# Six seven-product pairs in every block, and one PSUM bank used for two sums in turn

## The chip, the core and the metric

The kernel runs on one core of a Trainium2 chip. The metric is the device time of one execution in microseconds. The engines are called TensorE (PE), VectorE (DVE), ScalarE (ACT), GpSimd (POOL) and SyncE (SP); POOL and SP also issue transfers, each from a queue in order.

## The reference

Two layers of a bidirectional encoder on 256 tokens of width 4096, all in float32:

```python
for l in range(DEPTH):                       # DEPTH = 2
    h = rmsnorm(x, norm_w[l])
    proj = h @ w_in[l]                       # 4096 x 11264
    aq, ak, av, ag, rq, rk, rv, rg = jnp.split(proj, SPLIT_POINTS, axis=-1)
    a_out = silu(ag) * gqa_attention(rope(norm(aq)), rope(norm(ak)), av)       # 16 heads
    r_out = silu(rg) * rmsnorm(bidirectional_retention(rope(rq), rope(rk), rv)) # 8 heads
    x = x + jnp.concatenate([a_out, r_out], axis=-1) @ w_out[l]                # 4096 x 4096
return rmsnorm(x, final_norm)
```

Nearly all of the arithmetic is in the products with `w_in` and `w_out`.

## The kernel before, in words

**Blocks.** The columns of `w_in` are taken in 11 blocks of 1024 per layer and those of `w_out` in 4, so there are 30 blocks. The 4096 rows of a weight matrix are 16 *pairs* of 128-row slices (p = 0 to 15). In a block each pair contributes a 2 x 2 product of matrices: two halves of the tokens, two slices of the rows, two halves of the columns. It is done in eight products, or in Winograd's way in seven.

**A product** is brought close to float32 by three matmuls of 512 columns: the high parts of weights (`whi`) and operand (`x8h`, `x7h`), high by low, low by high. L1472 issues the two with the weights' high part, L1482 the one with the low part. A product is added into one of the sums M1 to M8, each in a PSUM bank; the eighth bank is called `ps` and belongs to attention and retention. M1 to M7 have a bank each.

**Seven or eight.** `SEVEN` lists the pairs done in seven products in the w_in blocks, `MORE` those added in the w_out blocks. The eight-product pairs use the sums of the others: `EIGHT_PRODUCTS` spreads them over M2 to M5, which needs the operand's difference (the *third* operand, `x3`, high and low). `PLAIN_PRODUCTS` needs no difference but a sum M8 of its own; with `plain` blocks M8 lies in `ps`. `NATIVE` pairs (1 and 0) are taken in the very first block as plain float32 matmuls (L1466), straight from the operand as it comes.

**Pages.** The weights of a pair are used as pages. An eight-product pair has pages A and B, of four products each. A seven-product pair has A, T, B and U, of 2, 2, 1 and 2 products; T and U are sums that DVE makes from the raw weights (`wsum`). For a page ACT makes `whi` and DVE makes `wlo`. `RING` = 5 pages are in work: when PE has used a page up, the fifth after it is begun. The raw weights come by SP's queue into `RAWS` buffers (L458). Pages of `FAR_PAIRS` (their B page) are *far*: ACT makes the high part and its negative, and POOL adds the raw weights to it by an accumulating transfer from DRAM (`flo`, L516); `FAR` buffers hold them. `pages_of` gives the order within a group, which is one seven-product pair and the eight-product pairs up to the next.

**Operands.** `split_pair` makes a pair's operand for a *stage* (in, out, in, out): high and low parts, for a seven-product pair also four sums and a negative (`xf`), for the others the third operand. The stage's inputs are the results of the stage before: chunks of two pairs, the last two of which (pairs 12 to 15) stay on the chip and come last. In stage 0 the thirds are made later (`DEFER`), after the `plain` blocks.

**The order of work** is written out by a planner inside the kernel while it is built. It keeps an estimate of PE's, DVE's and ACT's time and gives tasks (gates, rotary embedding, attention, retention, residual and norm) a place between the weights' work where `room` says that there is slack. `STEP_S`, `MARGIN`, `RUSH`, `EARLY`, `ADD_AHEAD`, `NEED`, `PE_REST`, `TIGHT_A`, `TIGHT_B`, `BANK_REST` and `SPLITS` are its constants. `PAGES` buffers of 4 KB per partition serve the tasks. At a block's end `combine` adds the banks into `ca` and `cb`; the sums of pair 15 are sorted to the end in `LAST_ORDER`. `TOGETHER` is how many products of a page have their high matmuls issued before their low ones.

**The start.** 20 warm-up matmuls run first (L1705). `first_rows(0)` loads the rows of x, transposed, for pair 1, then the first weights, then those for pair 0; ACT scales them (`full`, by `nw`) in the order of `NATIVE`, pair 1 before pair 0. In the order before, `pages_of` puts pair 1's pages ahead of pair 0's.

Of the kernel before, what the change touches and what calls it, by code (L numbers as in the profile page):

```python
# [17 lines left out]
P = 128  # L18
# [9 lines left out]
NB = 512  # L28
# [6 lines left out]
ALL = slice(None)  # L35
PAGES = 9
RAWS = 5

RING = 5
FAR = 1  # L40

STEP_V = 1.6
STEP_S = 1.3

# [9 lines left out]
FAR_LANDING = 11.0  # L54
MARGIN = 0.2

RUSH = 1.5

EARLY = 0.7

ADD_AHEAD = 2.5

NEED = {"ak": 4, "ag": 3, "rk": 4, "rg": 4}

PE_REST = 1.5

TIGHT_A = 4
TIGHT_B = 7

# [3 lines left out]

SPLITS = 3

START = 1

SEVEN = (0, 3, 6, 9, 12)

MORE = (1,)  # L80

# [5 lines left out]

PLAIN = 2

DEFER = (0,)  # L90

FAR_PAIRS = (2, 5, 8, 11, 14)

# [79 lines left out]
EIGHTS = [_p for _p in range(NP) if _p not in SEVENS[1]]  # L173

GROUPS = [[tuple(range(_a, _b)) for _a, _b in zip(_s, _s[1:] + (NP,))] for _s in SEVENS]


def pages_of(group, first=False):

    order, one = [], group[:1]  # L180
    rest = group[1:]
    if first:
        order += [(_p, _k) for _p in NATIVE if _p in group for _k in (PAGE_A, PAGE_B)]
        one = [_p for _p in one if _p not in NATIVE]
        rest = [_p for _p in rest if _p not in NATIVE]
    one = [(_p, _k) for _p in one for _k in (PAGE_A, PAGE_T, PAGE_B, PAGE_U)]
    rest = [(_p, _k) for _p in rest for _k in (PAGE_A, PAGE_B)]
    turns = TURNS if group[-1] == NP - 1 else "0123"
    for _i, _v in enumerate(one):
        order += [_v] + [rest.pop(0) for _j in turns if _j == str(_i) and rest]  # L190
    return order + rest
# [21 lines left out]

EASY = ("M7",)


BANK_REST = 0.8
APART = 0.0

TOGETHER = 4  # L220

OTHER = True

TURNS = "0123"

# [47 lines left out]
def hybrid_encoder(  # L273
# [318 lines left out]
    def dead_room():  # L592

        if not rooms:
            e, o = len(EIGHTS), len(SEVENS[1])
            kinds = {
                "x3": ("x3", e, [P, 2, 2, P], "p k s t -> p (k s t)"),
                "x8h": ("x8h", e, [P, 2, SEQ], "p k s -> p (k s)"),
                "x8l": ("x8l", e, [P, 2, SEQ], "p k s -> p (k s)"),
                "x7h": ("x7h", o, [P, 7, P], "p k t -> p (k t)"),  # L600
                "x7l": ("x7l", o, [P, 7, P], "p k t -> p (k t)"),
            }
            for p in range(NP):
                if p not in EIGHTS:
                    rooms.extend(kinds[v] for v in ("x7h", "x7l"))
                else:
                    rooms.extend(kinds[v] for v in ("x3", "x8h", "x8l")[: 3 if p in EIGHTS[2:] and p not in DELAYED else 1])
        tag, bufs, shape, flat = rooms.pop(0)
        return t(ap, shape, tag, bufs, F32R).rearrange(flat)[:, :NB]
# [18 lines left out]
    def split_pair(p, v, whole, stage):  # L628
# [39 lines left out]
        else:  # L668
            if p in EIGHTS:
                hi = t(ap, [P, 2, SEQ], "x8h", len(EIGHTS), F32R)  # L670
                lo = t(ap, [P, 2, SEQ], "x8l", len(EIGHTS), F32R)
                g = t(ap, [P, 2, 2, P], "x3", len(EIGHTS), F32R)
                g = [g[:, k] for k in range(2)]
            else:
                both = [t(ap, [P, 7, P], v, len(SEVENS[1]), F32R) for v in ("x7h", "x7l")]
                hi, lo = (v[:, 0:4, :].rearrange("p (i m) t -> p i (m t)", m=MT) for v in both)
                g = [v[:, 4:6, :] for v in both]
            g4 = [tokens(v) for v in g]
# [8 lines left out]
            for h, w, src in pieces:  # L687
                ve.tensor_sub(w, src, f32(h))
            if stage in DEFER:
# [671 lines left out]
    def block(after_pair, phase, then, first_order=False, order=LAST_ORDER, last=None, plain=False, hurried=False):  # L1361
# [12 lines left out]
        if plain:  # L1374
            order = PLAIN_ORDER
            bank[0] = True
# [11 lines left out]
        flat = [v for v in flat if not at_end(v)] + end  # L1388
        banks = BANKS if plain else BANKS[:-1]
        first = {b: next(i for i, v in enumerate(flat) if v[0] == b) for b in banks}  # L1390
# [5 lines left out]
        acc, pages, c = {}, {}, []  # L1396
        done = []
        def begin_product(n, name, p, index, k, h):
# [90 lines left out]
    def combine(bank, acc, c):  # L1489
# [109 lines left out]
    def last_combine(res):  # L1599
# [10 lines left out]
        def last(bank, acc, c):  # L1610
# [4 lines left out]
            if bank == "M6":  # L1615
                combine(bank, acc, c)
                ve.tensor_add(cb[:, 1, :], ca[:, 1, :], res[1, 1])
                ve.tensor_add(ca[:, 1, :], ca[:, 1, :], res[0, 1])
                ve.tensor_add(cb[:, 0, :], cb[:, 0, :], res[1, 0])
                ve.tensor_add(ca[:, 0, :], ca[:, 0, :], res[0, 0])  # L1620
            elif bank == "M2":
                combine(bank, acc, c)
                square(0, c, 0)
            elif bank == "M5":
                ve.tensor_add(cb[:, 0, :], cb[:, 0, :], acc["M5"])
                ve.tensor_add(cb[:, 1, :], cb[:, 1, :], acc["M5"])
                square(1, c, 1)
# [213 lines left out]
```

## Time and profile before

| | |
|---|---|
| time, median of 3 runs | 2622.15 us (2621.75 to 2622.28) |
| span of the profiled execution, first to last instruction | 2619.4 us, 2.75 us below the median of the runs; the page gives no other time for it |
| PE busy | 2599.9 us (99%), 11725 matmuls |
| DVE, ACT, POOL busy | 2168.9 (83%), 1805.0 (69%), 373.9 us (14%) |
| moved by DMA | 683.95 MB, mean 261 GB/s |
| granted clock of PE | 0.998 |

Matmuls are pipelined: the profile shows one of 512 columns as 0.39 us, but they start closer together than that, so a pace is read from start to start. `M` stands for all of M1 to M7. L258 is the helper through which all DVE and ACT work is issued, so its rows are told apart by their tiles.

### The profile page before, as it was taken

Reading aid. Unit: us, or ns where it says so; the run is one execution under the profiler, and the core shown is the slowest. Engines: PE = TensorE matmul, PEld = TensorE weight load, DVE = VectorE, ACT = ScalarE, POOL = GpSimd, SP = SyncE. Lnnn points to the kernel's source line nnn. Section 1 sums busy time; section 2 is a strip of 40 time slices with the busy share of each in tenths; the row PEclk is TensorE's granted clock in tenths of the full one; section 3 lists DMA queues with packets and bytes.
Section 4 is the critical chain, followed back from the end, with each engine's and each line's share of the span. In section 5 each row is a group of like instructions: output and inputs, shape, how many; then the busy total and the mean of one; then the engine's idle time right before and its main releaser. Section 6 shows DMA issues by size and latency. Waiting matters only on the chain.

```text
span 2619.4 us, 34550 instructions
## 1 busy us (share of the span) xinstructions
PE 2599.9 (99%) x11725; PEld 2153.7 (82%) x11725; DVE 2168.9 (83%) x2684; ACT 1805.0 (69%) x2576; POOL 373.9 (14%) x510
## 2 busy tenths in 40 slices
PE   9999999999999999999999999999999999999998
PEld 7888888888888888888878888888888888888886
DVE  8898887888778898877888878987887688987876
ACT  8766776666666788656886666776676567876555
POOL 0012221220111101111111111221110111010000
PEclk9999999999999999999999999999999999999999
DMA  8979989887878787988888888988877887788886
GB/s 306 292 257 297 284 257 287 274 270 240 247 229 258 225 252 237 283 269 269 301 251 262 271 286 268 278 270 282 280 228 218 249 259 237 224 255 270 242 261 221
DMA packets 201122, 683.95 MB, mean 261 GB/s; under 512 B 24176, under 2 KB 30832, under 8 KB 200944
## 3 DMA queue, kind: packets, MB, share of 16 engines
q1 hardware_dynamic: 147760, 521.27, 57.2%
q0 software_dynamic: 53184, 160.46, 26.3%
q8 instruction: 92, 1.51, 0.2%
q14 instruction: 86, 0.70, 0.1%
HBM read 637.60 MB, written 44.04 MB: 260 GB/s over the span
## 4 chain that ended last, share of the span: by engine, by line
PE 90%; DMA 1%; DVE 1%; issue 0%; ACT 0%; POOL 0%; POOLq 0%; DVEq 0%; ACTq 0%
PE M L1472 58%; PE M L1482 29%; PE ps L988 1%; PE ps L989 1%; PE ps L987 1%; DMA flo<-in_w_in 1%; DMA x7h<-in_w_out 0%; DVE wlo L258 0%; DVE ca L258 0%; DVE cb L258 0%; ACT flo L258 0%; ACT fhi L258 0%; ACT whi L258 0%; ACT x L258 0%; DVE xf L258 0%
## 5 line engine op out<-in xcount | busy, mean ns | idle before, releaser
L258 ACT CAST whi<-wraw 128x1024 fp32r<-128x1024 f32 (+1 forms) x808 | 768.0, 961 | 468.0 <-PE M L1472 318.7
L258 DVE TENSOR_TENSOR wlo<-wraw,whi 128x1024 fp32r<-128x1024 f32 (+1 forms) x808 | 887.6, 1110 | 234.0 <-ACT whi L258 226.2
L1472 PE MATMUL M<-whi,x8h 128*128 128x512 f32 x1340 | 521.8, 389 | 0.0
L1472 PE MATMUL M<-whi,x8l 128*128 128x512 f32 x1340 | 521.4, 389 | 0.0
L1472 PE MATMUL M<-whi,x7h 128*128 128x512 f32 x1265 | 493.2, 390 | 2.8 <-DVE ca L258 2.6
L1472 PE MATMUL M<-whi,x7l 128*128 128x512 f32 x1265 | 492.4, 389 | 0.0
L258 ACT CAST whi<-wsum 128x1024 fp32r<-128x1024 f32 x314 | 329.8, 1050 | 142.3 <-PE M L1472 109.2
L1482 PE MATMUL M<-wlo,x8h 128*128 128x512 f32 x1340 | 420.8, 389 | 0.0
L258 DVE TENSOR_TENSOR wlo<-wsum,whi 128x1024 fp32r<-128x1024 f32 x314 | 382.6, 1219 | 36.7 <-ACT whi L258 33.6
L1482 PE MATMUL M<-wlo,x7h 128*128 128x512 f32 x1265 | 408.5, 389 | 2.0 <-DVE wlo L258 2.0
L1472 PEld LDWEIGHTS M<-whi,x8l 128*128 128x128 f32 x1340 | 251.6, 188 | 52.3 <-issue 0.2
L1472 PEld LDWEIGHTS M<-whi,x8h 128*128 128x128 f32 x1340 | 251.5, 188 | 52.0 <-ACT full L258 0.2
L1482 PEld LDWEIGHTS M<-wlo,x8h 128*128 128x128 f32 x1340 | 250.5, 188 | 50.7
L1472 PEld LDWEIGHTS M<-whi,x7h 128*128 128x128 f32 x1265 | 237.5, 188 | 55.1 <-DVE ca L258 3.8
L1482 PEld LDWEIGHTS M<-wlo,x7h 128*128 128x128 f32 x1265 | 237.2, 188 | 51.6 <-DVE wlo L258 2.9
L1472 PEld LDWEIGHTS M<-whi,x7l 128*128 128x128 f32 x1265 | 237.5, 188 | 48.8
L1472 PE MATMUL M<-whi,x 128*128 128x512 f32 x840 | 258.8, 389 | 0.0
L516 POOL DMA_DIRECT2D flo<-in_w_in x108 | 96.7, 896 | 1045.3 <-ACT flo L258 965.6
L258 ACT CAST fhi<-wraw 128x1024 fp32r<-128x1024 f32 (+1 forms) x148 | 154.7, 1045 | 103.0 <-PE M L1472 97.7
L258 DVE TENSOR_TENSOR wsum<-wraw 128x1024 f32<-128x1024 f32 x157 | 191.2, 1218 | 24.2 <-DMA wraw<-in_w_out 15.6
L1472 PEld LDWEIGHTS M<-whi,x 128*128 128x128 f32 x840 | 156.9, 188 | 32.2 <-ACT whi L258 0.2
L1472 PE MATMUL M<-fhi,x8h 128*128 128x512 f32 x440 | 171.3, 389 | 0.0
(307 smaller groups left out, 3280.5 us busy)
## 6 DMA issues: line engine op xcount, KB each, us to landing
wraw<-in_w_in SPq DMA_DIRECT2D x700, 512.0 KB, 5.1
wraw<-in_w_out SPq DMA_DIRECT2D x256, 512.0 KB, 5.3
flo<-in_w_in POOLq DMA_DIRECT2D x108, 512.0 KB, 8.2
flo<-in_w_out POOLq DMA_DIRECT2D x38, 512.0 KB, 8.7
full<-next_dram POOLq DMA_DIRECT2D x18, 512.0 KB, 7.6
p_dram<-room POOLq DMA_DIRECT2D x64, 128.0 KB, 4.7
pT<-p_dram POOLq DMA_DIRECT2D x16, 512.0 KB, 5.9
next_dram<-room POOLq DMA_DIRECT2D x40, 128.0 KB, 6.8
```

What stands on the lines that cost most here:

```text
L258: return call(out, *args, **kwargs)
L516: nc.gpsimd.dma_start(g.lo[h], g.src[0][:, h, :], accum_op=ALU.add)
L987: nc.tensor.matmul(out, a[0], b[0], start=start, stop=False)
L988: nc.tensor.matmul(out, a[0], b[1], start=False, stop=False)
L989: nc.tensor.matmul(out, a[1], b[0], start=False, stop=stop)
L1472: nc.tensor.matmul(acc[name], a[i], g.hi[h], start=m == first[name] and not i, stop=False)
L1482: nc.tensor.matmul(acc[name], a, g.lo[h], start=False, stop=m == final[name])
```

## The change

Pairs 0, 1, 4, 5, 9 and 10 become the seven-product pairs in all blocks (before: 0, 3, 6, 9, 12 in w_in, and 1 as well in w_out). Eight-product pairs below `CUT` = 10 (2, 3, 6, 7, 8) keep `EIGHT_PRODUCTS` and a third operand. Those from 11 on use `PLAIN_PRODUCTS`. Their sum M8 takes M5's bank: when M5 is complete (pair 10), ACT copies it to a tile `m5`, and the bank is begun anew. Only the first block is wholly plain, with M8 in `ps` (before: two). The sums that are complete early are combined in the last 20 products. Far pages are those of seven pairs instead of five, in two places instead of one; raw buffers go from five to four and task buffers from nine to ten. In the last group the pages of pairs 11 to 15 come after all pages of pair 10.

```diff
-PAGES = 9
-RAWS = 5
+PAGES = 10
+RAWS = 4
-FAR = 1
+FAR = 2
-STEP_S = 1.3
+STEP_S = 1.5
-MARGIN = 0.2
-RUSH = 1.5
-EARLY = 0.7
-ADD_AHEAD = 2.5
-NEED = {"ak": 4, "ag": 3, "rk": 4, "rg": 4}
-PE_REST = 1.5
-TIGHT_A = 4
-TIGHT_B = 7
+MARGIN = 0.0
+RUSH = 2.0
+EARLY = 1.3
+ADD_AHEAD = 2.0
+NEED = {"ak": 5, "ag": 3, "rk": 4, "rg": 5}
+PE_REST = 1.2
+TIGHT_A = 0
+TIGHT_B = 3
-SPLITS = 3
-START = 1
-SEVEN = (0, 3, 6, 9, 12)
-MORE = (1,)
+SPLITS = 2
+START = 2
+SEVEN = (0, 1, 4, 5, 9, 10)
+MORE = ()
+CUT = 10
-PLAIN = 2
+PLAIN = 1
-FAR_PAIRS = (2, 5, 8, 11, 14)
+FAR_PAIRS = (2, 3, 7, 8, 11, 13, 15)
...
+CROSSED = [_p for _p in EIGHTS if _p < CUT]
...
-    turns = TURNS if group[-1] == NP - 1 else "0123"
     for _i, _v in enumerate(one):
-        order += [_v] + [rest.pop(0) for _j in turns if _j == str(_i) and rest]
+        order.append(_v)
+        if rest and _i >= (0 if rest[0][0] < CUT else TURN):
+            order.append(rest.pop(0))
...
-            eight = PLAIN_PRODUCTS if plain else EIGHT_PRODUCTS
+            eight = EIGHT_PRODUCTS if _p in CROSSED and not plain else PLAIN_PRODUCTS
...
-LAST_ORDER = ("M3", "M5", "M4", "M2")
-FINAL_ORDER = ("M5", "M2", "M3", "M4")
-PLAIN_ORDER = ("M3", "M8", "M4", "M2")
+LAST_ORDER = ("M3", "M8", "M4", "M2")
+FINAL_ORDER = ("M8", "M2", "M3", "M4")
+ENDING = 20
-BANK_REST = 0.8
+BANK_REST = 1.0
-TOGETHER = 4
+TOGETHER = 2
-TURNS = "0123"
+TURN = 3
...
             if n == first[name]:
-                acc[name] = t(pm, [P, NB], "ps" if name == "M8" else name)
+                if name == "M8" and not plain:
+                    now.wait(acc["m5_at"])
+                acc[name] = t(pm, [P, NB], name if name != "M8" else "ps" if plain else "M5")
...
-            if n == final[name]:
-                finished.append((name, partial(last or combine, name, acc, c)))
+            if n == final[name] and name == "M5" and not plain:
+                acc["m5"] = t(sp, [P, NB], "m5")
+                ac.copy(acc["m5"], acc["M5"])
+                acc["m5_at"] = ac.until + PASS
+            elif n == final[name]:
+                (finished if n >= len(flat) - ENDING else early).append((name, partial(last or combine, name, acc, c)))
+            if early and n >= len(flat) - ENDING:
+                finished.extend(early)
+                early.clear()
...
         if bank == "M6":
             ve.tensor_add(cb[:, 0, :], ca[:, 0, :], acc["M6"])
             ve.tensor_add(ca[:, 1, :], cb[:, 0, :], acc["M7"])
-            if "M8" in acc:
-                combine("M5 and M6", acc, c)
+            m5 = acc.get("m5", acc["M5"])
+            ve.tensor_add(cb[:, 1, :], ca[:, 1, :], m5)
+            ve.tensor_add(cb[:, 0, :], cb[:, 0, :], m5)
         elif bank == "M8":
             ve.tensor_add(cb[:, 1, :], cb[:, 1, :], acc["M8"])
-            free_bank()
-        elif bank == "M5 and M6" or bank == "M5" and "M8" not in acc:
-            ve.tensor_add(cb[:, 1, :], ca[:, 1, :], acc["M5"])
-            ve.tensor_add(cb[:, 0, :], cb[:, 0, :], acc["M5"])
+            if "m5" not in acc:
+                free_bank()
```

More of the change, by code (lines that the diff above doesn't have):

```diff
@@ L596, in dead_room @@
             kinds = {
-                "x3": ("x3", e, [P, 2, 2, P], "p k s t -> p (k s t)"),
+                "x3": ("x3", len(CROSSED), [P, 2, 2, P], "p k s t -> p (k s t)"),
                 "x8h": ("x8h", e, [P, 2, SEQ], "p k s -> p (k s)"),
@@ L605, in dead_room @@
                     rooms.extend(kinds[v] for v in ("x7h", "x7l"))
-                else:
-                    rooms.extend(kinds[v] for v in ("x3", "x8h", "x8l")[: 3 if p in EIGHTS[2:] and p not in DELAYED else 1])
+                elif p in EIGHTS[2:] and p not in DELAYED:
+                    rooms.extend(kinds[v] for v in ("x8h", "x8l"))
+                if p in CROSSED:
+                    rooms.append(kinds["x3"])
         tag, bufs, shape, flat = rooms.pop(0)
@@ L671, in split_pair @@
                 lo = t(ap, [P, 2, SEQ], "x8l", len(EIGHTS), F32R)
-                g = t(ap, [P, 2, 2, P], "x3", len(EIGHTS), F32R)
-                g = [g[:, k] for k in range(2)]
             else:
@@ L676, in split_pair @@
                 hi, lo = (v[:, 0:4, :].rearrange("p (i m) t -> p i (m t)", m=MT) for v in both)
-                g = [v[:, 4:6, :] for v in both]
+            g = []
+            if p in CROSSED:
+                g = t(ap, [P, 2, 2, P], "x3", len(CROSSED), F32R)
+                g = [g[:, k] for k in range(2)]
             g4 = [tokens(v) for v in g]
@@ L688, in split_pair @@
                 ve.tensor_sub(w, src, f32(h))
-            if stage in DEFER:
+            if not g:
+                pass
+            elif stage in DEFER:
                 thirds.append(Lane(None))
@@ L1374, in block @@
         if plain:
-            order = PLAIN_ORDER
             bank[0] = True
@@ L1388, in block @@
         flat = [v for v in flat if not at_end(v)] + end
-        banks = BANKS if plain else BANKS[:-1]
+        banks = BANKS
         first = {b: next(i for i, v in enumerate(flat) if v[0] == b) for b in banks}
@@ L1396, in block @@
         acc, pages, c = {}, {}, []
-        done = []
+        done, early = [], []
         def begin_product(n, name, p, index, k, h):
@@ L1616, in last @@
                 combine(bank, acc, c)
-                ve.tensor_add(cb[:, 1, :], ca[:, 1, :], res[1, 1])
+                ve.tensor_add(cb[:, 1, :], cb[:, 1, :], res[1, 1])
                 ve.tensor_add(ca[:, 1, :], ca[:, 1, :], res[0, 1])
@@ L1623, in last @@
                 square(0, c, 0)
-            elif bank == "M5":
-                ve.tensor_add(cb[:, 0, :], cb[:, 0, :], acc["M5"])
-                ve.tensor_add(cb[:, 1, :], cb[:, 1, :], acc["M5"])
+            elif bank == "M8":
+                combine(bank, acc, c)
                 square(1, c, 1)
```

## The prediction

> **What bounds the kernel now.** I read the page first, then the waits of TensorE (PE), the chain, the timeline of the start, the groups by line and shape, and last the windows with their DMA share.
>
> ```profile
> span 2619.4 us, 34550 instructions
> ...
> PE 2599.9 (99%) x11725; PEld 2153.7 (82%) x11725; DVE 2168.9 (83%) x2684; ACT 1805.0 (69%) x2576; POOL 373.9 (14%) x510
> ...
> PE 90%; DMA 1%; DVE 1%; issue 0%; ACT 0%; POOL 0%; POOLq 0%; DVEq 0%; ACTq 0%
> ```
>
> ```profile
> PE M L1472 <- DVE ca L258: 2.6, 4, 1.0
> PE M L1482 <- DVE wlo L258: 2.0, 2, 1.7
> ...
> PE M L1482 <- DMA flo<-in_w_in: 0.9, 2, 0.6
> ...
> PE M L1482 <- DMA x7h<-in_w_out: 0.4, 1, 0.4
> ```
>
> PE is busy for 99% of the span, and its waits in steady work (columns: us in total, times, longest) come to 5.9 us. A full PE can be made faster only by fewer or shorter matmuls, and there is little else to win. Pace and ends:
>
> ```profile
> 191.02 1.81 PE M L1472 x8
> ...
> 195.10 1.81 PE M L1472 x8
> ```
> ```profile
> 21.35 0.79 PE L1472 MATMUL M<-whi,x8h 128*128 128x512 f32 x1
> ...
> 2607.26 0.39 PE L1482 MATMUL M<-x7h,x8h 128*128 128x512 f32 x1
> ```
>
> Between the two chain rows lie a page of four products and one of two, 18 matmuls in 4.08 us, so 0.2267 us for one of 512 columns and 0.680 us for a product of three. The last matmul starts at 2607.3; what follows to the span's end (about 12 us) is the tail. The count checks the code: a w_in block has 5 x 7 + 11 x 8 = 123 products, a w_out block 6 x 7 + 10 x 8 = 122, the first block 124 (pair 0 is taken as eight), 16 of them native with two records each. That is 22 x 123 + 1 + 8 x 122 = 3683 products, and 3667 x 3 + 32 + 672 small + 20 warm-up = 11725, the page's count.
>
> **The change part by part.**
>
> *Products.* With six seven-product pairs everywhere, 21 w_in blocks fall from 123 to 122. The first block stays at 124, since pairs 0 and 1 are both native there and four sevens are left, as before. The w_out blocks stay at 122. So 21 products, 63 matmuls, 63 x 0.2267 = **-14.3 us**, directly on the path. The Trainium skill, "TensorE: Matmul & The Clock Gate", Part 1, gives N / 2.4 GHz plus about 2.5 ns for a warm matmul, 215.7 ns at N = 512; by it the term would be 13.6 us. The trace's 226.7 ns does not agree and decides.
>
> *Vector and scalar work of the weights.*
>
> ```profile
> L258 DVE TENSOR_TENSOR wlo<-wraw,whi 128x1024 fp32r<-128x1024 f32 x643 | 781.7, 1219 | 224.8 <-ACT whi L258 217.4 <-PE M L1482 2.7 <-PE M L1472 2.4
> L258 DVE TENSOR_TENSOR wlo<-wsum,whi 128x1024 fp32r<-128x1024 f32 x314 | 382.6, 1219 | 36.7 <-ACT whi L258 33.6 <-PE M L1482 3.0
> L258 DVE TENSOR_TENSOR wsum<-wraw 128x1024 f32<-128x1024 f32 x157 | 191.2, 1218 | 24.2 <-DMA wraw<-in_w_out 15.6 <-DMA wraw<-in_w_in 8.2 <-PE M L1466 0.3
> L258 DVE TENSOR_TENSOR wlo<-wraw,whi 128x512 fp32r<-128x512 f32 x165 | 113.1, 686 | 9.2 <-ACT whi L258 8.7
> L258 DVE TENSOR_TENSOR wsum<-wsum,wraw 128x512 f32<-128x512 f32 x157 | 108.7, 692 | 5.4
> L258 DVE TENSOR_TENSOR wsum<-wraw,wsum 128x512 f32<-128x512 f32 x157 | 107.4, 684 | 0.3 <-issue 0.2
> ...
> L258 DVE TENSOR_TENSOR cb<-cb,M 128x512 f32<-128x512 f32 x61 | 41.3, 678 | 8.4 <-PE M L1482 8.4
> ```
> ```profile
> L258 ACT CAST whi<-wsum 128x1024 fp32r<-128x1024 f32 x314 | 329.8, 1050 | 142.3 <-PE M L1472 109.2 <-DVE wsum L258 30.6 <-PE M L1482 1.2
> L258 ACT ACTIVATE flo<-fhi 128x1024 fp32r<-128x1024 f32 x146 | 155.0, 1061 | 5.2 <-PE M L1482 0.6
> ...
> L258 ACT CAST whi<-wraw 128x512 fp32r<-128x512 f32 x165 | 101.9, 618 | 54.7 <-PE M L1472 48.4 <-DMA wraw<-in_w_out 5.6 <-ACT x L258 0.7
> ```
>
> A seven-product pair costs DVE 1.22 + 0.68 + 0.69 (sums) + 3 x 1.22 + 0.69 (lows) = 6.94 us and ACT 3 x 1.05 + 0.62 = 3.77 us; an eight-product pair 2.44 and 2.10. A far page moves 1.22 us of DVE to 1.06 us of ACT and a second transfer. There are 157 sevens now (the x157 row) and 178 after, and 148 far pages now (30 x 5 - 2) and 208 after. DVE: 21 x 4.50 - 60 x 1.22 = +21 us; eight instead of seven bank sums in about 29 blocks add 29 x 0.68 = +20; 22 third operands fewer (42 now, 5 in each of four stages after) take back about as much. ACT: 21 x 1.67 + 60 x 1.06 + 29 copies of M5 = about +115. DVE stays near 84%, ACT goes to some 74%. Cover: PE's own 82 us per block. I charge **0**, but the order matters (rivals).
>
> *Seven-product pairs early.* Stage changes are where PE waits now:
>
> ```profile
> 1310.00:1397.00 87.00, 84.00 (x366) 68.25 (x367) 72.05 (x95) 68.87 (x110) 8.58 (x10) 1.00 0.85 254
> ```
>
> PE (third number) is 3.0 us short there, the first block of layer 2, behind DVE. The pairs that come last out of a stage, 12 to 15, now need a seven's sums and three third operands; after, only a high and a low part. I take **-1.5** of these 3.0. Against it, the second block must have the five delayed third operands (it was plain before): bounds 0 and 5 x (4 x 0.42 DVE + 0.40 ACT) = 10, where a 256-column subtraction is 0.42 (row below); nearest to the 0.4 to 0.8 us that the block changes lose now, I take **+1.5**.
>
> ```profile
> L258 DVE TENSOR_TENSOR full<-full 128x256 f32<-128x256 f32 x22 | 9.3, 425 | 0.8
> L258 ACT COPY ca<-M 128x512 f32<-128x512 f32 x30 | 17.1, 570 | 0.0
> ```
>
> *M5's bank.* M5 ends in pair 10's second page; ACT copies it (0.57 us), and M8 begins in the bank in pair 11's first page. Between lie one matmul of M7, three of M2, six of M6 and M4 and two of M3: 12 x 0.2267 = 2.7 us. What waits behind is PE itself. Cost **0** while ACT is less than 2.1 us behind; 29 x 0.57 = 17 us if the whole copy is exposed. At a block's end one bank sum goes (M8 takes one where M5 took two), which frees banks sooner; the very last sum, M4's, is the same, so the tail stays.
>
> *Transferred lows: two places, seven pages.*
>
> ```profile
> q1 hardware_dynamic: 147760, 521.27, 57.2%
> q0 software_dynamic: 53184, 160.46, 26.3%
> ```
> ```profile
> flo<-in_w_in POOLq DMA_DIRECT2D x108, 512.0 KB, 8.2
> ```
> ```profile
> 349.00:436.00 87.00, 87.00 (x404) 72.82 (x404) 72.84 (x87) 60.88 (x97) 18.66 (x28) 1.00 0.89 274
> 1048.00:1135.00 87.00, 87.00 (x386) 72.03 (x385) 71.35 (x76) 53.10 (x62) 12.38 (x17) 1.00 0.92 280
> 1397.00:1484.00 87.00, 87.00 (x385) 72.05 (x384) 71.11 (x92) 55.48 (x74) 13.73 (x17) 1.00 0.93 274
> ```
> ```profile
> SPq L458 <- DVE wlo L258: 1434.9, 554, 10.1
> ```
>
> A far page is begun when the one two places earlier is used up. The shortest such lead is from the end of 15B to 3B, 26 products or 17.7 us, against 8.2 us to landing; the 0.9 us of waits for flo goes: **-0.9**. Each transfer also takes a place in POOL's queue, in order with the stores and fetches of the tasks; POOL is 14% busy. Price on the DMA engines: q0's 26.3% of 2619 us is 689 us for 160.5 MB; charging its 83 MB of plain copies at q1's rate (57.2% = 1498 us for 521 MB, 2.9 us per MB, 239 us) leaves 450 us for 148 accumulating transfers, 3.0 us each. Two more per block are 6 us, 0.07 of a window's share. At the same time raw buffers fall from five to four. SP waits for a free buffer (1435 us behind wlo alone), not for the wire, so landing is mostly ahead of need; but late raws will be more frequent. Bounds 0 and the DMA rival below; I take **+2.0**, two more waits of the size of the first row's longest (1.0).
>
> *The first block.*
>
> ```profile
> 5.11 0.91 ACT L258 ACTIVATE full<-full,nw 128x256 f32<-128x256 f32 x2 [2.86 <-DMA full<-in_xT]
> 7.34 0.91 ACT L258 ACTIVATE full<-full,nw 128x256 f32<-128x256 f32 x2 [1.32 <-DMA full<-in_xT]
> ```
> ```profile
> 1.09 4.45 PE L1705 MATMUL ps<-junk 128*128 128x256 bf16 x20 [1.09 <-DVE junk L258]
> 6.07 2.08 PE L1466 MATMUL M<-fhi,full 128*128 128x512 f32 x2 [0.53 <-ACT full L258]
> 7.94 1.91 PE L1466 MATMUL ps<-fhi,full 128*128 128x512 f32 x2
> ```
>
> Now both native pairs are in the first group, so pair 1 goes first, whose rows of x are loaded and scaled first (ACT until 6.02). After, pair 0 is alone in its group and goes first, but `first_rows` and `NATIVE` still bring pair 1's rows first: pair 0's scaling ends at 8.25. PE is gapless from there to the first split page, so the delay passes on: **+2.2**. The first native records lie 0.85 us apart (two before 7.94 and two after), the later ones 0.43; with a longer pause after the warm-up this slow stretch may last longer: 0 to 1.7 us, I take **+0.5**. The clock gate of the same skill page agrees in kind (Part 1: half rate until a free-running window of 3.4 us has been busy): a restart at 8.3 us would be slow for 3.4 to 6.8 us and lose 1.7 to 3.4, where 1.8 are lost now.
>
> *The last block* has three far pages among the pairs with kept halves (11, 13, 15) where two were, and x7h was late by 0.4 us: **+0.5**. `TOGETHER` 2 asks for a four-product page's low 0.9 us sooner, and the planner's constants move tasks only; with wlo late twice in all, **0**.
>
> Sum: -14.3 - 1.5 + 1.5 - 0.9 + 2.0 + 2.2 + 0.5 + 0.5 = **-10.0 us**. The profiled span goes from 2619.4 to 2609.4; the median lies 2.75 us above the span, so 2622.15 becomes **2612.2**.
>
> **The rivals.**
>
> *Gapless.* All steady waits go (5.9 us) and nothing new comes: -14.3 + 2.7 - 5.9 and hence about 2605. For it, DVE's lighter stage ends. Chance 0.12.
>
> *DVE too dense.* Pairs 9 and 10 are 14 products, 9.5 us, with 13.9 us of DVE work; the ring of five pages lets 9's pages and 10's first be done ahead. From the end of 9's first page to pair 11 are 12 products, 8.2 us, in which DVE owes 1.38 + 1.22 + 0.69 + 1.22 + 1.22 = 5.7. It decides if tasks put more than 2.5 us there: three steps of 1.2 are 1.2 too many, and in one block of three that is 29 / 3 x 1.2 = 12 us, hence 2624, no change. For it, DVE's 83%; against it, the planner gives tasks time only where weights have slack. Chance 0.11.
>
> *The DMA engines become the bound* (the slower side). Shares of 0.89 to 0.93 plus 0.07 are 0.96 to 1.00. If no more than the 0.93 seen with a full PE can be had, a block like 349 to 436 takes 0.96 / 0.93 of its time, 2.8 us more; in the eight attention blocks 22 us, hence about 2632. It decides where two more transfers need more than the idle share. Against it, SP's waits for buffers. Chance 0.09.
>
> *M5's copy exposed* in every block: +17, 2629. Chance 0.04. That the product count does not fall has next to no chance: it follows from the lists.
>
> **How the numbers follow.** Forecast 0.64 (2605 to 2617 by itself), gapless 0.12, DVE 0.11, DMA 0.09, copy 0.04. About 0.2% (5.2 us) is what a measurement can tell from no change. Faster: 0.64 + 0.12 less 0.02 for a forecast case that misses the bound, 0.74. Same: 0.11 + 0.02 = 0.13. Slower: 0.13. The range 2605 to 2620 leaves out the slower 0.13, half of the DVE case and a little below.
>
> **What would show it.** PE x11662, wsum x178, flo x208 right the counts; first native matmul at 8.3 and not 6.1; no waits of M L1472 on ACT m5; waits on flo gone; PE full in the block from 1300. Wrong would be PE waits for wlo or whi once per block (the DVE case), with raw waits on ACT and a DMA share at 0.97 and more (the DMA case).

## The result and the profile after

| | before | after |
|---|---|---|
| median of 4 runs each, same chip | 2622.22 us (2621.75 to 2623.68) | 2828.52 us (2824.15 to 2830.39) |
| ratio | 1 | 1.0782 [1.0767, 1.0797] |
| span of the profiled execution | 2619.4 us | 2822.4 us (its time: 2824.15) |

The kernel is 206 us slower; 10 us faster was forecast, and the range ended at 2620. The page of after, with the rows that answer to those of before (M L1491 is what M L1472 was, L1501 the former L1482, L264 the former L258):

```profile
span 2822.4 us, 34752 instructions
...
PE 2667.4 (95%) x11662; PEld 2166.4 (77%) x11662; DVE 2188.2 (78%) x2709; ACT 1897.4 (67%) x2689; POOL 423.5 (15%) x571
...
q1 hardware_dynamic: 147760, 521.27, 52.7%
q0 software_dynamic: 61968, 191.92, 30.4%
...
PE 53%; DMA 21%; DVE 13%; ACT 9%; issue 5%; POOL 0%; ACTq 0%; SPq 0%; DVEq 0%; POOLq 0%
```

The 63 matmuls went. But PE carries only 53% of the chain where it carried 90%, and DMA, which had 1%, carries 21%. Next the waits of PE in the trace of after (total us, times, longest):

```profile
PE M L1491 <- ACT whi L264: 54.6, 32, 5.0
PE M L1491 <- DVE ca L264: 19.7, 11, 2.8
PE M L1491 <- ACT m L264: 16.1, 10, 3.2
PE ps L999 <- DVE pTl L264: 12.1, 8, 3.7
...
PE M L1491 <- ACT x8h L264: 4.7, 2, 2.7
...
PE M L1485 <- ACT full L264: 3.7, 1, 3.7
```

The first row had no counterpart before: PE waits for the high part of a weight page. The next view says why ACT was late with it. Waits of ACT, first in the trace of before, then in that of after:

```profile
ACT whi L258 <- DMA wraw<-in_w_out: 84.6, 37, 5.1
ACT whi L258 <- DVE wsum L258: 38.2, 21, 2.8
ACT whi L258 <- DMA wraw<-in_w_in: 37.4, 22, 4.5
```
```profile
ACT whi L264 <- DMA wraw<-in_w_in: 205.5, 130, 4.4
ACT whi L264 <- DVE wsum L264: 193.0, 97, 5.1
ACT whi L264 <- DMA wraw<-in_w_out: 91.1, 50, 5.9
```

ACT stands still for a raw w_in page 130 times instead of 22, and for a weight sum, which needs two raw pages, 97 times instead of 21. Two windows of after, one in the attention blocks and one for the first block of layer 2, which now begins at 1409 (us, then busy PE, PEld, DVE, ACT and POOL, the granted clock, the DMA share, GB/s):

```profile
349.00:436.00 87.00, 83.48 (x371) 67.47 (x370) 67.66 (x83) 59.03 (x93) 15.45 (x23) 0.98 0.86 267
```
```profile
1409.00:1496.00 87.00, 76.29 (x322) 59.07 (x320) 64.46 (x84) 72.55 (x121) 9.53 (x11) 1.00 0.81 237
```

PE is no longer full and the DMA engines are less busy than before (0.86, not 0.89): what is late is not the wire.

Measured from one matmul's start to the next, and counting what a gap has above 0.2267 us (0.1167 for 256 columns), PE lost 10.5 us in all before and 222 us after. That is 7 us a block in the mean, with two blocks of the 30 near nothing and the most in one 14 us. The largest places are the first page of pair 6 (69 us), attention and retention products (42), page B of pair 0 (23), and the first page of pair 11, which follows the copy of M5 (23). So 222 - 10.5 less 14.3 for the matmuls and 3 for the later start give about +200 of the 206.

A stall costs twice. One, in the timeline of PE of after:

```profile
1169.78 0.61 PE L1501 MATMUL M<-wlo,x7h 128*128 128x512 f32 x2
1173.56 0.79 PE L1491 MATMUL M<-whi,x8h 128*128 128x512 f32 x1 [3.17 <-ACT whi L264]
1174.15 0.63 PE L1491 MATMUL M<-whi,x8l 128*128 128x512 f32 x1
1174.58 0.63 PE L1491 MATMUL M<-whi,x8h 128*128 128x512 f32 x1
```
```profile
1172.46 1.56 ACT L264 CAST whi<-wraw 128x1024 fp32r<-128x1024 f32 x2 [5.89 <-DMA wraw<-in_w_out]
```

ACT waited 5.9 us for a page to land, PE 3.2 us for ACT, and the matmuls after it start 0.43 us apart instead of 0.227 until 1179. About 173 matmuls of after run at that pace, 0.2 us longer each, which makes some 35 us of the 222.

### The profile page after: what moved, and what is told of

It reads as the page before. It is cut to its first block, busy times and chain, and to the rows that moved or that the text cites. A ratio compares the mean times of both kernels' runs of the same rounds, so it can differ in the third digit from the quotient of the medians.

```text
span 2822.4 us, 34752 instructions
## 1 busy us (share of the span) xinstructions
PE 2667.4 (95%) x11662; PEld 2166.4 (77%) x11662; DVE 2188.2 (78%) x2709; ACT 1897.4 (67%) x2689; POOL 423.5 (15%) x571
## 3 DMA queue, kind: packets, MB, share of 16 engines
q0 software_dynamic: 61968, 191.92, 30.4%
## 4 chain that ended last, share of the span: by engine, by line
PE 53%; DMA 21%; DVE 13%; ACT 9%; issue 5%; POOL 0%; ACTq 0%; SPq 0%; DVEq 0%; POOLq 0%
PE M L1491 33%; PE M L1501 17%; DMA wraw<-in_w_in 14%; DVE wlo L264 6%; DMA wraw<-in_w_out 5%; ACT whi L264 4%; DVE wsum L264 2%; ACT fhi L264 2%; DVE cb L264 1%; PE ps L1000 1%; PE ps L999 1%; DVE ca L264 1%; DMA cb<-in_x 1%; PE ps L998 1%; ACT ca L264 1%
## 5 line engine op out<-in xcount | busy, mean ns | idle before, releaser
L264 DVE TENSOR_TENSOR wlo<-wraw,whi 128x1024 fp32r<-128x1024 f32 (+1 forms) x748 | 808.2, 1087 | 331.8 <-ACT whi L264 325.8
L264 ACT CAST whi<-wraw 128x1024 fp32r<-128x1024 f32 (+1 forms) x748 | 696.2, 940 | 484.6 <-DMA wraw<-in_w_in 205.5
L1491 PE MATMUL M<-whi,x8h 128*128 128x512 f32 x1365 | 545.0, 399 | 24.8 <-ACT m L264 16.1
L1491 PE MATMUL M<-whi,x8l 128*128 128x512 f32 x1365 | 543.1, 398 | 1.7 <-DVE x8l L264 1.7
L264 ACT CAST whi<-wsum 128x1024 fp32r<-128x1024 f32 x356 | 372.7, 1047 | 253.4 <-DVE wsum L264 190.5
L1491 PE MATMUL M<-whi,x7h 128*128 128x512 f32 x1246 | 491.8, 395 | 30.1 <-DVE ca L264 19.7
L1491 PE MATMUL M<-whi,x7l 128*128 128x512 f32 x1246 | 489.2, 393 | 1.8 <-DVE x7l L264 1.8
L264 DVE TENSOR_TENSOR wlo<-wsum,whi 128x1024 fp32r<-128x1024 f32 x356 | 433.7, 1218 | 73.4 <-ACT whi L264 70.7
L1501 PE MATMUL M<-wlo,x8h 128*128 128x512 f32 x1365 | 457.4, 397 | 2.0 <-DVE wlo L264 1.7
L1501 PE MATMUL M<-wlo,x7h 128*128 128x512 f32 x1246 | 414.4, 394 | 2.9 <-DVE wlo L264 2.1
L1491 PEld LDWEIGHTS M<-whi,x8h 128*128 128x128 f32 x1365 | 262.6, 192 | 86.6 <-ACT m L264 20.8
L522 POOL DMA_DIRECT2D flo<-in_w_in x152 | 136.1, 898 | 1253.7 <-ACT flo L264 1140.8
L1501 PEld LDWEIGHTS M<-wlo,x8h 128*128 128x128 f32 x1365 | 262.8, 193 | 58.7 <-DVE wlo L264 4.1
L1491 PEld LDWEIGHTS M<-whi,x8l 128*128 128x128 f32 x1365 | 262.8, 193 | 58.2 <-DVE x8l L264 2.7
L1491 PEld LDWEIGHTS M<-whi,x7h 128*128 128x128 f32 x1246 | 236.4, 190 | 89.7 <-ACT whi L264 27.1
L264 DVE TENSOR_TENSOR wsum<-wraw 128x1024 f32<-128x1024 f32 x178 | 216.6, 1217 | 114.1 <-DMA wraw<-in_w_in 57.0
L1501 PEld LDWEIGHTS M<-wlo,x7h 128*128 128x128 f32 x1246 | 234.6, 190 | 59.7 <-DVE wlo L264 11.8
L1491 PE MATMUL M<-fhi,x8h 128*128 128x512 f32 x705 | 275.1, 390 | 0.0
L1491 PE MATMUL M<-fhi,x8l 128*128 128x512 f32 x705 | 274.9, 390 | 0.0
L1491 PEld LDWEIGHTS M<-whi,x7l 128*128 128x128 f32 x1246 | 236.0, 189 | 50.0 <-DVE x7l L264 2.2
L264 ACT CAST fhi<-wraw 128x1024 fp32r<-128x1024 f32 x208 | 217.0, 1043 | 78.9 <-PE M L1491 31.5
L1501 PE MATMUL M<-flo,x8h 128*128 128x512 f32 x705 | 237.0, 389 | 0.1
```

Source lines behind the costliest of these rows:

```text
L264: return call(out, *args, **kwargs)
L522: nc.gpsimd.dma_start(g.lo[h], g.src[0][:, h, :], accum_op=ALU.add)
L1491: nc.tensor.matmul(acc[name], a[i], g.hi[h], start=m == first[name] and not i, stop=False)
L1501: nc.tensor.matmul(acc[name], a, g.lo[h], start=False, stop=m == final[name])
```

## The experiments

Two groups of theories. For the whole loss: four raw buffers are too few to cover the landing of a page; seven-product pairs side by side ask too much of DVE at once; the far transfers fill the DMA engines. Then, for what is left with five raw buffers: the planner's constants, a backlog of the attention chain (theory 4), DVE's load as such (theory 5), or the way early sevens hold raw buffers and want their operands sooner (theory 6). Times with no interval are of one run, beside one or more of the kernel before on the same chip.

### Raw buffers

The changed kernel with one raw buffer more, paid for with a task buffer. With nine task buffers the sums at a block's end must be taken there in every block, hence the last lines.

```diff
-PAGES = 10
-RAWS = 4
+PAGES = 9
+RAWS = 5
-                if name == order[0] or n == len(flat) - 1:
-                    follow(True)
+            if n == final[name] and (name == order[0] or n == len(flat) - 1):
+                follow(True)
```

> The changed kernel with five raw buffers again (task buffers 10 to 9 to make room for it, and the bank sums forced out at the block's end as in the kernel before, without which nine task buffers do not build). Theory 1, raw buffers: two seven-product pairs in a row hold all four raw buffers until their sums are made, so the next load starts late and ACT waits for its landing; with a fifth most of that goes: ACT's waits for raw weights fall from some 300 us to under 120, time 2630 to 2710. Theory 2, dense DVE work: waits for raw weights go but PE still waits for whi and wlo: over 2780. Theory 3, DMA engines full by 60 more accumulating transfers: over 2780, since the transfers are the same.

Measured: 2735.24 us (before 2623.87), in the direction of theory 1 but above its range. It also speaks against the theory of full DMA engines: the far transfers are the same, and the time falls by 93 us. The same edit without the fifth raw buffer (`PAGES = 9`, `RAWS = 4`) separates the two sizes:

> The control to a_raws5: the changed kernel with nine task buffers and the bank sums forced at a block's end, but with its four raw buffers. It says what the fifth raw buffer alone is worth in the change's order. If the task buffers do not matter: 2815 to 2845, so that the fifth raw buffer is worth some 90 us. If nine task buffers cost as such: above 2860, and the fifth raw buffer is worth more than 93 us.

Measured: 2881.26 (before 2624.86). So in the order of the change the fifth raw buffer is worth 2881.3 - 2735.2 = 146 us, and the tenth task buffer (with the sums at a block's end as they were) 2881.3 - 2828.5 = 53. The mirror image is the kernel before with one raw buffer fewer and nothing else:

```diff
-RAWS = 5
+RAWS = 4
```

> The kernel before with four raw buffers instead of five, nothing else. Theory 1: it loses too, less than the changed kernel since its seven-product pairs lie three apart: 2640 to 2720, with ACT's waits for raw weights at two to three times the 122 us of before. Theories 2 and 3: within 5 us of 2622.

Measured: 2771.72, +148 us, more than was expected. Waits of ACT in that trace, then in the one with five buffers in the change's order:

```profile
ACT whi L258 <- DMA wraw<-in_w_in: 258.4, 134, 6.1
ACT whi L258 <- DMA wraw<-in_w_out: 172.9, 65, 8.6
```
```profile
ACT whi L264 <- DVE wsum L264: 150.1, 86, 4.4
ACT whi L264 <- DMA wraw<-in_w_in: 86.5, 69, 2.9
...
ACT whi L264 <- DMA wraw<-in_w_out: 36.0, 35, 2.9
```

Taking a buffer away brings the waits for landings, giving it back removes most of them, and both orders price it at 146 to 148 us. This part is shown.

### The order of the pairs, and the far transfers

```diff
-SEVEN = (0, 1, 4, 5, 9, 10)
-FAR_PAIRS = (2, 3, 7, 8, 11, 13, 15)
+SEVEN = (0, 2, 4, 6, 8, 10)
+FAR_PAIRS = (1, 3, 7, 9, 11, 13, 15)
```

> The changed kernel with the seven-product pairs at 0, 2, 4, 6, 8, 10, so that one eight-product pair lies between any two (far pages of 1, 3, 7, 9, 11, 13, 15); four raw buffers as in the change; the first block has one product fewer. Theory 1: a seven-product pair leaves two raw buffers for its neighbour, so part of the loss goes: 2650 to 2730. Theory 2: most goes, 2610 to 2660. Theory 3: over 2780.

Measured: 2893.83, 65 us slower still, where theories 1 and 2 both had it faster. With four raw buffers, setting the sevens apart does not help; why it is slower was not taken apart.

```diff
-FAR = 2
-FAR_PAIRS = (2, 3, 7, 8, 11, 13, 15)
+FAR = 1
+FAR_PAIRS = (2, 6, 8, 12, 14)
```

> The changed kernel with five far pages per block (pairs 2, 6, 8, 12, 14) in one place, as many accumulating transfers as the kernel before, four raw buffers. Theory 3: the loss goes, under 2680. Theory 1: it stays, 2780 to 2860. Theory 2: some 20 to 60 us worse than the changed kernel, since DVE has two more lows per block.

Measured: 2850.18. With 60 transfers fewer it is no faster. By itself this run settles nothing, since with the single place PE waits 96 us for far pages, which it does not in after:

```profile
PE M L1501 <- DMA flo<-in_w_in: 73.0, 26, 7.7
...
PE M L1501 <- DMA flo<-in_w_out: 22.7, 13, 3.8
```

### The planner's constants

The constants of before (`STEP_S`, `MARGIN`, `RUSH`, `EARLY`, `ADD_AHEAD`, `PE_REST`, `TIGHT_A`, `TIGHT_B`, `SPLITS`, `BANK_REST`) in the change with five raw buffers:

> The changed kernel with five raw buffers and nine task buffers as in the run before, and with the planner's constants of the kernel before (STEP_S, MARGIN, RUSH, EARLY, ADD_AHEAD, PE_REST, TIGHT_A, TIGHT_B, SPLITS, BANK_REST). Theory 1a, the rest of the loss (112 us) is the planner's: with MARGIN 0 and PE_REST 1.2 it places tasks without slack, and any delay of ACT or DVE reaches PE: 2640 to 2690. Theory 1b, the rest is the order with two seven-product pairs in a row: within 20 us of 2735.

Measured: 2753.84 (before 2621.37), 19 us slower than without. The constants of after in the kernel before:

> The kernel before with the change's planner constants alone. Theory 1a: 2640 to 2720. Theory 1b: within 10 us of 2622.

Measured: 2654.90, +33 us. In the kernel before with a sixth seven (next part):

> The kernel before with six seven-product pairs in all blocks (0, 1, 3, 6, 9, 12) and the change's planner constants, five raw buffers. Theory 4, backlog: in b_six the tasks lose their place to the weights' work, fall behind and are caught up with PE waiting, 27 us of stalls in each first w_out block (pair 8's operand, from retention) and 6 in blocks 6 and 7; constants that leave tasks less slack to ask for (MARGIN 0, EARLY 1.3) let them run sooner: 2640 to 2690, with the first w_out block under 100 us. If the constants only add the small stalls that they added to the kernel before (33 us): 2730 to 2750.

Measured: 2710.15, +2. The set of after is worse in the order of before, better in that of the change, and makes no difference with the sixth seven, against both forecasts there. So the constants do not explain what the change loses. `TOGETHER = 4` in the change with five raw buffers:

> The changed kernel with five raw buffers and nine task buffers, and with the high matmuls of four products of a page ahead of their low ones, as before (TOGETHER 4), so that a low part is needed 0.9 us later in each page of four. If lows come late by under a microsecond often: 10 to 40 us less than 2735. Otherwise within 10 us of it.

Measured: 2743.21, +8, no clear difference (four runs of the next kernel lie 10 us apart).

### The sixth seven-product pair alone

The product part of the change, in the kernel before, with its five raw buffers and far pages:

```diff
-SEVEN = (0, 3, 6, 9, 12)
-MORE = (1,)
+SEVEN = (0, 1, 3, 6, 9, 12)
+MORE = ()
```

> The kernel before with pairs 0, 1, 3, 6, 9, 12 as seven-product pairs in all blocks (the set that its w_out blocks have already), five raw buffers, M5 and the planner untouched: the product term alone, 21 products fewer. If the term of the sum is right and only the change's other parts cost: 14.3 us of matmuls less, some 3 us more at the start (pair 0's pages go first while pair 1's rows are loaded first), so 2609 to 2614. If a sixth seven-product pair itself overloads DVE in the w_in blocks: 2622 or more, with waits for wlo in the blocks with attention.

Measured: 2708.58 (2706.41 to 2716.07, 4 runs) to 2621.37 (7 runs), ratio 1.0336 [1.0317, 1.0355]. The 63 matmuls are gone, and yet it is 87 us slower; by itself the saving costs more than it brings. Start to start, 27 us each are lost in blocks 11 and 26, the first of each w_out stage, which last 115.9 us instead of 85.9 and 86.6. That is about half of what PE loses; another 9 us go in the first block, where PE waits 6.2 us for a far page, and the rest in small parts elsewhere. First row of the waits of PE:

```profile
PE M L1472 <- ACT x L258: 31.9, 6, 11.4
```

The operand of the next stage is late, above all that of pair 8. It is made by tasks that run beside the blocks before. Is the attention chain behind (theory 4)? The planner's estimates of a store and a fetch were cut so that chains are planned closer:

```diff
-STORE = 7.0
-FETCH = 13.0
+STORE = 5.0
+FETCH = 9.0
```

> b_six with the planner's allowances for transfers cut (FETCH 13 to 9, STORE 7 to 5; the semaphores stay). Each attention task waits out some three fetches and two stores, so its chain gets about 16 us shorter. Theory 4, the attention tasks run one after the other and take 104 to 115 us each in b_six where a block takes 89, so that all that follows falls behind: with a chain of about 95 us the backlog and most of the 27 us in the first w_out blocks go: 2620 to 2660. If the loss is DVE's load as such: 2700 to 2720.

Measured: 2712.21. The last attention product of layer 1 ended at 628 us instead of 664 in the run with the sixth seven, but block 11 stalled 27.7 us as before. So it is not the attention chain that is late there, and theory 4 falls in that form. More pairs at once (`AT_ONCE = 3`):

> b_six with three tasks begun at a time instead of two (AT_ONCE). Theory 4: attention tasks may overlap where nine task buffers allow it; the buffers seldom do (an attention task needs six), so a part of the loss at most: 2660 to 2710. If the loss is DVE's load: 2700 to 2720.

Measured: 2706.69, no effect. The fetch estimates in the kernel before:

> The control: the kernel before with the same cut allowances. Its attention tasks just keep pace (89 to 92 us each), so a shorter chain gains nothing there, and a transfer that lands later than allowed holds PE: 2615 to 2640.

Measured: 2659.09 to 2623.0, ratio 1.0139 [1.0117, 1.0161]. A seventh seven in w_out alone, `MORE = (1, 10)`, 24 matmuls fewer:

> The kernel before with a seventh seven-product pair (10) in the w_out blocks, where no attention task runs: 8 products fewer, 8 x 0.68 = 5.4 us. If the loss of the sixth pair in w_in is the tasks' backlog alone: 2615 to 2620. If DVE or the raw buffers cannot bear pairs 9 and 10 both in seven products in these blocks (raw weights were waited for there already): 2622 to 2660.

Measured: 2642.28 to 2623.0, ratio 1.0078 [1.0062, 1.0095]. The steady w_out blocks take 82.3 us instead of 83.0, but blocks 11 and 26 lose 9.6 and 10.6. Again a saving on PE is paid back where a w_out stage begins.

### DVE's load by itself

The kernel before, its products, transfers and the number of its buffers untouched; DVE computes some weight sums twice (same values) in the w_in blocks:

```diff
+                                 one.extra = w is w_in and not start and one.pair in (3, 9)
...
+                if g.extra:
+                    ve.tensor_sub(self.v, self.a, self.b[:, 0:1, :].to_broadcast([P, 2, NB]))
...
+                if g.extra:
+                    ve.tensor_add(self.u[:, 0, :], self.a[:, 1, :], self.v[:, 0, :])
+                if g.extra and g.pair == 3:
+                    ve.tensor_sub(self.u[:, 1, :], self.u[:, 0, :], self.b[:, 1, :])
```

> The kernel before with VectorE sums done twice in every block but the first (about four and a half microseconds of them in a w_in block, in the pairs that have seven-product tiles); products, buffers, transfers and the order of the pairs stay as before, so the output does too. If VectorE's load at the end of a stage is what costs the kernel with a sixth seven-product pair its 87 us (theory 5), this kernel loses in the same place: the blocks that begin the w_out products, 11 and 26, stall by 15 to 30 us each, and the time is at least 2680. If the loss comes from how the sixth pair holds raw buffers and delays the operands of the early pairs (theory 6), the load alone finds room in the slack of VectorE (about 10 us of 87 in a block) and the time stays under 2640. Between the two: both have a share.

Measured: 2740.87 (before 2623.03), and with pair 9 alone:

> The kernel before with the doubled VectorE sums in pair 9 alone: 21 blocks x (1.22 + 0.69) = 40 us more VectorE work, where the run with pairs 3 and 9 had 95 us more and lost 118 us. If every microsecond of VectorE work in a w_in block costs PE about 1.25 us (no slack left at all), the time is about 2670. If there is a slack and a knee (theory 5 with a threshold), it stays within 10 us of the kernel before, under 2635.

Measured: 2669.28 (before 2621.07). Busy rows of the pages with the sixth seven, the half load and the full load, and the longest wait of PE in the last:

```profile
PE 2616.1 (97%) x11662; PEld 2156.0 (80%) x11662; DVE 2249.3 (83%) x2791; ACT 1832.1 (68%) x2620; POOL 368.6 (14%) x511
```
```profile
PE 2613.0 (98%) x11725; PEld 2159.7 (81%) x11725; DVE 2206.1 (83%) x2726; ACT 1808.7 (68%) x2576; POOL 370.5 (14%) x510
```
```profile
PE 2639.1 (96%) x11725; PEld 2170.8 (79%) x11725; DVE 2257.7 (82%) x2789; ACT 1808.8 (66%) x2576; POOL 367.1 (13%) x510
```
```profile
1067.63 1.62 PE L1479 MATMUL M<-whi,x 128*128 128x512 f32 x2 [9.52 <-ACT x L258]
```

Against the 2168.9 us of before, DVE has 37.2 us more in the half load and 88.8 in the full one; the time rises by 48.2 and 117.8, that is by 1.30 and 1.33 for each. The sixth seven brings 80.4 us and loses 87.2 + 14.3 = 101.5 on other things than products: 1.26 for each. The agreement is in part luck, since about 12 of the 101.5 us are a later start and the first block, which the two loads do not touch.

The same blocks stall: the full load loses 28.3 and 27.4 us in blocks 11 and 26, above all at the first pages of pairs 8, 10 and 14, as with the sixth seven. The half load loses 20.3 and 19.7 there, at pairs 14 and 10; that is about the 19 to 21 us of DVE work added to the 10 or 11 blocks ahead of each. The full load adds twice that, and shows the other half of its loss in the w_in blocks. The doubled sums also hold their raw pages longer: ACT waits 54.3 us for raw w_in pages in the half load and 121.9 in the full one (before 37.4), so the full load is not DVE's alone. With that said, DVE work alone brings a loss of this kind in these blocks, and no threshold is seen: theory 5 fits the sixth seven, though it is not shown that nothing else is in its 87 us.

It could be thought that DVE is simply used up there. In the trace of before, in the 40 us in which block 10 ends and block 11 begins (at 973.6), it nearly is:

```profile
960.00:1000.00 40.00, 40.00 (x181) 33.23 (x180) 39.10 (x55) 29.61 (x41) 2.27 (x3) 1.00 0.69 210
```

DVE is busy for 39.1 of 40 us and PE is full (36.0 and 35.1 us of DVE in the 40 us on either side). But with the sixth seven DVE has room while block 11 (from 995.2) stalls, 41.9 us busy in 50:

```profile
1010.00:1060.00 50.00, 39.36 (x169) 31.99 (x168) 41.92 (x61) 33.48 (x52) 2.82 (x4) 0.90 0.60 192
```

The longest wait there, 10.6 us for pair 8's operand, ends behind a fetch. These are rows of POOL, ACT and PE of that run:

```profile
1036.48 0.86 POOL L516 DMA_DIRECT2D flo<-in_w_out  x1 [20.29 <-ACT flo L258]
1037.44 0.56 POOL L800 DMA_DIRECT2D full<-next_dram  x1
```
```profile
1047.87 1.70 ACT L258 ACTIVATE full<-full,nw 128x256 f32<-128x256 f32 x4 [4.39 <-DMA full<-next_dram]
```
```profile
1051.61 1.63 PE L1472 MATMUL M<-whi,x 128*128 128x512 f32 x2 [10.60 <-ACT x L258]
```

POOL's queue stood 20.3 us before a far transfer, and the fetch of pair 8's rows came right behind it; it took 10.4 us to land, and then ACT and DVE needed 3.7 us. In the full load the 9.5 us wait ends in the same way: its fetch is issued at 1051.0, lands at 1063.5, and PE goes on at 1067.6. What PE waits for last is thus a fetch issued too late for its block, and not DVE itself. Whether it is late because tasks are given their places late, and whether an earlier fetch, or the idle time that DVE has in the earlier blocks of the stage (815 of 967 us are busy in before), would save the loss, was not tried.

Last, the change with five raw buffers and an eighth far page, meant to take 37 us off DVE (33 by the page):

```diff
-FAR_PAIRS = (2, 3, 7, 8, 11, 13, 15)
+FAR_PAIRS = (2, 3, 6, 7, 8, 11, 13, 15)
```

> The changed kernel with five raw buffers and nine task buffers (2735 us), with an eighth far page (pair 6) in each block: 30 low parts of 1.22 us leave VectorE (-37 us), 30 more on ScalarE (+32 us) and 30 more accumulating transfers. If VectorE's load sets the 113 us that this version has over the kernel before (theory 5), it falls by 30 us or more, to 2705 or less. If the place of the seven-product pairs and the order of the operands set it (theory 6), it stays within 15 us of 2735. If the far places are now too close, waits of PE for flo appear and it gets slower.

Measured: 2774.26, 39 us slower, with the reason in its first waits of PE:

```profile
PE M L1501 <- DMA flo<-in_w_in: 39.0, 15, 5.0
PE M L1491 <- ACT x7h L264: 21.9, 2, 11.9
PE M L1501 <- DMA flo<-in_w_out: 13.9, 5, 4.7
```

Pair 8's far page now comes too close behind pair 6's. The run doesn't tell whether the relief of DVE helps.

### The sum

| step | us |
|---|---|
| kernel before | 2622 |
| sixth seven alone | +87 |
| rest of the change (M5's bank, order, seven far pages, constants), five raw buffers | +27 |
| raw buffers five to four | +146 |
| task buffers nine to ten | -53 |
| changed kernel | 2829 |

Apart from the two kernels and the sixth seven, the steps are differences of single runs, and all depend on their order. What is in the +27 was not taken apart. Nor is it shown that the +87 keeps its size and cause there: the far pages had taken DVE's load back to 2187.7 us in that run, only 19 above before, and at 1.3 that is 24 of the 126 us (111 and the 14.3 saved) that this version loses. Its blocks 11 and 26 still lose 21 us each to late operands. So the cause of some 100 us of this version's loss stays open. No version ran faster than the kernel before.

## Why the prediction was wrong, step by step

*Raw buffers, the step that failed most.* The prediction put the loss of one at +2.0, because "SP waits for a free buffer (1435 us behind wlo alone), not for the wire, so landing is mostly ahead of need". The row says the opposite. If the loader always waits for a free buffer, the number of buffers decides how far ahead a page is asked for, and each one taken shortens that lead. The row that would have sized it:

```profile
wraw<-in_w_in SPq DMA_DIRECT2D x700, 512.0 KB, 5.1
```

With the 256 of w_out these are 956 pages in 2619 us, one in 2.74. At that rate five buffers allow 13.7 us from issue to release, four 11.0. Of that 5.1 go to landing, so the time for sums, casts and waiting in order falls from 8.6 to 5.9, while a seven must hold its first page until its second has landed and sums of both have run. The term of +2.0 measured 146 to 148 us. The SP rows of after show who else holds the buffers, the sums of the sevens and the casts of the far pages (before: 288.3 and 144.0). With five buffers in the change's order they are as large (524.6 and 514.2), so they belong to the order, and the missing buffer comes on top:

```profile
SPq L464 <- DVE wsum L264: 512.8, 170, 11.1
SPq L464 <- ACT fhi L264: 383.0, 176, 9.4
```

*Vector work at 0.* The amounts were right: DVE +19 us (+21 forecast), ACT +92 (about +115). The price was wrong. "DVE stays near 84%" is a mean over the span, and the cover named, PE's time in a block, was not free: with work added to DVE the operands of the next stage came late, and PE waited. Added DVE work cost 1.3 us of time per us in the order of before; the sixth seven alone, which the prediction had at -14.3 and nothing on the other side, cost 87 us net. The DVE rival was nearer in engine, but put it at pairs 9 and 10 and at 12 us; what stalled was the start of a w_out stage.

*Products at -14.3.* x11662 and the 0.227 us pace of undisturbed stretches are as forecast. The saving is there and is buried.

*Early sevens at -1.5, thirds at +1.5.* The first block of layer 2 was to have a full PE; it has 76.3 of 87 us where it had 84.0. Part of that is the missing raw buffer, but with five raw buffers the first block of layer 2 still loses 4.8 us (4.6 before) and the second block of layer 1 4.2 (1.1). So nothing was gained in the one, and the other, where the third operands are made, lost 3.1 us more, twice the term. Wrong.

*M5's copy at 0.* PE waited for it 16.1 us, in ten of 29 blocks and 1.6 us each. That it is nearly the 17 us bound is chance, since the bound had 0.57 us in every block: ACT is late with the copy by more. With five raw buffers it is 6.5. The rival named this price and had 0.04.

*Flo waits at -0.9.* Right: no wait of PE for flo is left in after, nor with five raw buffers. *Far transfers*: 30.4% of 2822 less 26.3% of 2619 us is 169 us for 60 more, 2.8 us each; 3.0 were forecast. The rival built on it fell: the mean share of both queues went from 83.5 to 83.1%, and the sign named for it, a share of 0.97, is reached in no window of 87 us (the most is 0.95). Its other sign, raw waits of ACT, came true with another cause.

*The start at +2.2* measured +3.15, by these rows of after (6.07 before):

```profile
8.26 0.91 ACT L264 ACTIVATE full<-full,nw 128x256 f32<-128x256 f32 x2 [2.90 <-DMA full<-in_xT]
```
```profile
9.22 2.08 PE L1485 MATMUL M<-fhi,full 128*128 128x512 f32 x2 [3.72 <-ACT full L264]
```

*Slow restart and last block, +0.5 each.* The 32 native matmuls take 14.9 us from the first one's start, 15.3 before, so the restart cost nothing more. No wait for a transferred x7h is left in after.

*Constants and `TOGETHER` at 0.* In the order of before the constants alone cost 33 us, in the change's order they gain 19 (single runs, on two chips whose runs of before differ by 2.5 us); the 8 us of `TOGETHER` are not clear of the scatter.

The rivals on the slower side stopped at 2632. None asked what happens if the loader's lead shrinks, though the change itself took a buffer away.

## What to carry to other kernels

A queue that waits for a free buffer all the time is not slack: multiply the number of buffers by the time between two loads, subtract the landing, and see what is left for the work on a page before taking one away. An engine's mean load over the span does not say what added work costs: here DVE was at 83%, and work added to it cost more than its own time, through operands that came late where a stage begins. So look at the start of the next stage, and at what its first operands wait for. In a kernel with PE at 99%, a matmul saved can be lost several times over to the work it adds to the engines that feed PE: here 14.3 us saved cost 101.5.

## What the runs showed of the hardware

One buffer of 512 KB out of five was worth 5.6% of the time (2623.9 to 2771.7), while the two queues took 83.5% of the DMA engines' time with five and 54.8 + 25.1 = 79.9% with four: on the average of the span the engines had room in both.

The clock falls after short stalls. In after, counted by what a gap has above the usual pace, 21 of 30 gaps of 2 us or more between matmuls were followed, within some 15 matmuls, by at least three, mostly about seven, at half pace, 0.43 us apart for 512 columns; of 35 gaps of 0.8 to 2 us, 7 were. Eleven of the 21 followed gaps of under 3 us. The Trainium skill, "TensorE: Matmul & The Clock Gate", Part 1, says the clock drops after at least one idle window of about 3.4 us; the half rate agrees with the trace (0.43 to 0.227; the granted clock is 0.5 in 25 stretches of 3.4 or 6.8 us while matmuls still run), the length of the pause does not.
